# Operand starts on 128-byte multiples and a reordered opening, in a fused two-block kernel

## Chip, core and metric

One core of a Trainium2 chip runs the whole program. The metric is the device time of one launch in microseconds; lower is better.

## The reference, cut to what matters

A sequence of 256 tokens of width 1024 goes through two models, one after the other, each of two layers. Everything is float32. A layer of the first model is a SwiGLU feed-forward, a mixer (retention, stick-breaking attention and a Mamba-2 scan side by side) and a second feed-forward; a layer of the second is a mixer of three attentions and a feed-forward. Each of these stages is preceded by a root-mean-square norm whose gain and shift come from a conditioning vector `c`:

```
mod = (silu(c) @ ada_w[l] + ada_b[l]).reshape(B, 3 * N_SUB, D_MODEL)[:, None]
u = modulate(rmsnorm(h, norm_ffn1[l]), mod[:, :, 0], mod[:, :, 1])
h = h + 0.5 * (1.0 + mod[:, :, 2]) * swiglu(u, ffn1_wg[l], ffn1_wu[l], ffn1_wd[l])
```

So there are ten stages, nearly all of their arithmetic in products of 256 tokens with weight matrices that are read once from HBM, and some 470 MB of weights in all.

## The kernel before, in words

**Products.** A float32 value x is split into H = x rounded to float32r and L = x - H, and a product is three matmuls in float32r (`mm3`, line 174): H·H, H·L, L·H. In a matmul one operand is loaded into the array (128 columns, a weight load, called PEld in the profile) and the other streams past it (up to 512 columns). The profile writes a matmul as out<-streamed,loaded: `A<-s,uH` streams a weight tile `s` past the activations `uH`, `A<-uH,s` streams activations past weights. For the feed-forward, `gemmB` (line 380) and `down` stream 512 weight columns past the activations `uH`/`uL` or `m`; `gemmA` (line 389) streams 256 activation columns. Plain float32 matmuls (attention scores and the like) are done in two passes, and transposes (`tr`, line 179) stream the identity past the tile.

**Weights.** `dma_next` (line 301) loads 512 KB units on SP's queue into tiles of tag s4. `prep_H` copies a unit to float32r on ACT (line 321), `prep_L` subtracts on DVE (line 185). The conditioning products are done on DVE: `ada_load` (line 501) brings 512 KB, `ada_dot` (line 506) multiplies by silu(c) and sums.

**Order.** Python runs the stages once and writes the instructions out in order. `pump` advances a planned clock by 216 ns a matmul and lets side lanes (transposes, attention, ada dots) step when their planned time has come. The opening (`prologue`) is written by hand in the order in which every engine is to run it: two outer products spread c over the partitions and ACT applies silu; the norms of the two halves of x; transposes of x; then for k = 0 to 7 the gain and shift of 128 features, their u, and the products of that k with four weight groups, each into a PSUM bank of its own.

**Memory.** Tiles come from pools, and a pool's tiles have tags. A tag has a fixed number of buffers that lie together; the tags of a pool lie one behind the other in the order of first use, each buffer rounded up to 32 bytes a partition. The constants' pool begins at byte 1152 and holds onesrow 512, h0 and h1 4096 each, vtab 1768 (1792), ident 512, mhalf 32, ctab 10496, ones 4 (32), and onesr, identr, nones 512 each. Behind it come the working tags, before the change in the order s4 (36 of 4096), cb (4096), sm (16 of 32), gs (8 of 32), v8 (3 of 32), uH and uL (8192 each), m2 (15 of 2048), then small ones. Summed up, s4 begins at byte 24256, which is 64 past a multiple of 128; uH, uL and m2 begin 32 past one. Slices of these tiles that go into products step by 512 bytes or multiples, so every s4 operand starts at 64, every u and m2 operand at 32 (modulo 128). `ident` starts at 0, `ltrir` (a small late tag) at 0.

Of the kernel before, what the change touches and what calls it, by code (L numbers as in the profile page):

```python
# [13 lines left out]
AF = mybir.ActivationFunctionType  # L14
ALU = mybir.AluOpType
# [4 lines left out]
D = 1024  # L20
FF = 2816
NJ = FF // 256
EPS = 1e-6
# [80 lines left out]
class K:  # L104
# [196 lines left out]
    def dma_next(self):  # L301
        i = self.dma_i
        k, src = self.plan[i]
        raw = self.m4([128, 1024])
        n = src.shape[1]
        self.nc.sync.dma_start(raw[:, :n], src)
        self.raws[i] = (raw, k, n // k)
        self.dma_i += 1
        self.raw_live += 1
# [5 lines left out]
    def prep_H(self):  # L315
        self.fill_dma()
        raw, k, wd = self.raws.pop(self.prep_i)
        n = k * wd
        H = self.m4([128, 1024], F32R)
        L = self.m4([128, 1024], F32R)  # L320
        self.nc.scalar.copy(H[:, :n], raw[:, :n])  # L321
        vh = H[:, :n].rearrange("p (k n) -> p k n", k=k)
        vl = L[:, :n].rearrange("p (k n) -> p k n", k=k)
        self.prepped[self.prep_i] = (vh, vl)
        self.prep_i += 1
        self.live += 1
        self.last_prep = self.now
        return H, L, raw, n
# [374 lines left out]

    def run(self):
        a, nc = self.a, self.nc
        self.ones_row = self.t([1, 128], "onesrow", 1, pool=self.cst)
        nc.vector.memset(self.ones_row, 1.0)
        crow = self.m4([1, 1024])
        nc.sync.dma_start(crow, a["c"])
        self.h = [self.t([128, 1024], f"h{i}", 1, pool=self.cst) for i in range(2)]  # L710
        x = a["x"].rearrange("o (t p) d -> (o t) p d", p=128)
        for tt in range(2):
            nc.sync.dma_start(self.h[tt], x[tt])
        self.vtab = self.t([128, NV], "vtab", 1, pool=self.cst)
        nc.sync.dma_start(self.vtab, a["vtab"])
        self.ident = self.t([128, 128], "ident", 1, pool=self.cst)
        make_identity(nc, self.ident)
        self.mhalf = self.t([128, 8], "mhalf", 1, pool=self.cst)
        nc.gpsimd.memset(self.mhalf, -0.5)
        self.ctab = self.t([128, NCST], "ctab", 1, pool=self.cst)  # L720

        ph = self.phase_list()
        for plan, _, _, _ in ph:
            plan()

        items = self.ada_plan()
        while items[0][0] != ph[0][2][0]:
            items.pop(0)
        with self.tc.manual_schedule():
            u = self.prologue(crow, items[:2])  # L730
        self.ones = self.t([128, 1], "ones", 1, pool=self.cst)
        nc.gpsimd.memset(self.ones, 1.0)
        self.onesr = self.t([128, 128], "onesr", 1, F32R, pool=self.cst)
        nc.scalar.copy(self.onesr, self.ones.to_broadcast([128, 128]))
        self.identr = self.t([128, 128], "identr", 1, F32R, pool=self.cst)
        nc.scalar.copy(self.identr, self.ident)
        self.nones = self.t([128, 128], "nones", 1, pool=self.cst)
        nc.gpsimd.memset(self.nones, -1.0)
        self.later(60.0, lambda: nc.sync.dma_start(self.ctab, a["ctab"]))
        self.filling = True  # L740
        self.fill_dma()
        self.ada = self.spawn([self.ada_gen(items[2:])], 4.0)
        pend = None

        for i, (_, body, _, gate) in enumerate(ph):
            last = i == len(ph) - 1
            xn = {}
            g = {}
            self.WH = 12 if body == self.ffn else 8
            self.pace = PACE[i]  # L750
            self.ada_ok = True
            for ev, accs in body(u, pend):
                if "gate" not in g:
                    g["gate"] = self.need(*gate)
                if ev in (0, 1):
                    self.hold = True
                    if last:
                        self.finish(ev, accs, g["gate"])
                        continue
                    ex = self.final_mod if ph[i + 1][2][0][0] == "b" and ph[i][2][0][0] == "a" else None  # L760
                    if ex:
                        self.fm = self.fm if hasattr(self, "fm") else self.final_mod_prep()
                    xn[ev] = self.fin_a(ev, accs, g["gate"], ex)
                elif ev == 2 and not last:
                    nu = self.new_u()
                    g["G"], g["S"] = self.need(*ph[i + 1][2][0]), self.need(*ph[i + 1][2][1])
                    self.fin_b(0, xn[0], nu, g["G"], g["S"])
            if not last:
                u = nu
                pend = (lambda xn1, nu, G, Sh: lambda: self.fin_b(1, xn1, nu, G, Sh))(xn[1], nu, g["G"], g["S"])  # L770

    def prologue(self, crow, items):


        nc = self.nc
# [3 lines left out]
        def issue(k, steps):  # L779
            for s in steps:  # L780
                if s == "a":
                    raws[k] = (self.ada_load(wg, k), self.ada_load(ws, k))
                else:
                    self.dma_next()
# [6 lines left out]

        self.cb = self.t([128, 1024], "cb", 1)
        self.cb_of = cn
        for nb in range(2):
            c = slice(nb * 512, nb * 512 + 512)
            p = self.pB()
            self.mm(p, self.ones_row, crow[:, c], True)
            self.act(self.cb[:, c], p, AF.Silu)


        ss = [self.sm([128, 2]) for _ in range(2)]
        xn = [self.m4([128, 1024]) for _ in range(2)]
        for t in ss:
            nc.gpsimd.memset(t, 0.0)
        self.act(xn[0], self.h[0], AF.Square, accum_out=ss[0][:, 0:1])
        nc.vector.scalar_tensor_tensor(xn[1], self.h[1], 1.0, self.h[1], op0=ALU.mult, op1=ALU.mult,
                                       accum_out=ss[1][:, 0:1])
        r = [self.rstd2(t) for t in ss]
        g = self.vtab[:, _VEC["nf1"]:_VEC["cw"]]
        self.ts(g, g, 32.0, ALU.mult)  # L810
        gb = self.t([128, 8], "gs", 8)
# [1 line left out]
        v8 = [self.t([128, 8], "v8", 3) for _ in range(2)]  # L813
        gs = [self.t([128, 8], "gs", 8) for _ in range(2)]

        def dot(k):
            self.ada_dot(raws[k][0], v8[0][:, k:k + 1])

        def scale(k):
            c = slice(k, k + 1)  # L820
            self.act(gs[0][:, c], v8[0][:, c], AF.Identity, scale=gain[:, c], bias=gb[:, c])
# [5 lines left out]
        for tt in range(2):  # L827
            self.act(xn[tt][:, 512:1024], self.h[tt][:, 512:1024], AF.Copy, scale=r[tt])
        xT = [self.m4([128, 4, 256]) for _ in range(2)]
        for q in range(4):  # L830
            p = (self.pT, self.pA)[q // 2]()
            for i in range(4):
                k, tt = q * 2 + i // 2, i % 2
                self.tr(p[:, i * 128:i * 128 + 128], xn[tt][:, k * 128:k * 128 + 128])
            dst = xT[q // 2][:, q % 2 * 2:q % 2 * 2 + 2].rearrange("p k n -> p (k n)")
            nc.scalar.copy(dst, p)

        u = self.new_u()
        self.WH = 12
# [2 lines left out]
        def products(k, j0):  # L842
            W = self.take()
            for b in range(2):
                for tt in range(2):
                    self.mm3(ps[j0 + b][tt], self.uap(u, tt, k), (W[0][:, b], W[1][:, b]), k == 0, k == 7)
            self.done()

        for k in range(8):
            c = slice(k, k + 1)  # L850
            self.ada_dot(raws.pop(k)[1], v8[1][:, c])
            w = self.prep_H()
            self.act(gs[1][:, c], v8[1][:, c], AF.Identity, bias=bs[:, c])
            if k < 7:
                dot(k + 1)
            t = self.m2([128, 2, 128])
            self.act(t, xT[k // 4][:, k % 4].rearrange("p (t n) -> p t n", t=2), AF.Identity, scale=gs[0][:, c],
                     bias=gs[1][:, c])
            nc.scalar.copy(u[0][:, :, k], t)
            self.sub(u[1][:, :, k], t, u[0][:, :, k].bitcast(F32))  # L860
            if k < 7:
                scale(k + 1)
            w2 = self.prep_H()
            self.prep_L(w)
            products(k, 0 if k < 7 else 2)
            self.prep_L(w2)
            products(k, 2 if k < 7 else 0)
            if k + 3 < 8:
                issue(k + 3, "aww")
            else:  # L870
                self.dma_next()
                self.dma_next()
# [973 lines left out]
```

## Time and profile before

| | |
|---|---|
| median of 3 runs | 1977.92 us (1977.2 to 1978.46) |
| the profiled execution | 1974.64 us, of which the span of the profile is 1972.9 us |
| PE busy | 1924.5 us of the span |
| mean granted TensorE clock | 0.996 of 2.4 GHz |
| DMA | 471.18 MB, 239 GB/s on average |

Busy times are of the profiled execution; times in a timeline are from the start of the span. A matmul's duration in the profile is longer than the distance to the next one's start, because matmuls are pipelined: what a matmul costs is that distance, called its pitch here.

### The profile page before, as it was taken

Reading aid. Unit: us, or ns where it says so; the run is one execution under the profiler, and the core shown is the slowest. Engines: PE = TensorE matmul, PEld = TensorE weight load, DVE = VectorE, ACT = ScalarE, POOL = GpSimd, SP = SyncE. Lnnn points to the kernel's source line nnn. Section 1 sums busy time; section 2 is a strip of 40 time slices with the busy share of each in tenths; the row PEclk is TensorE's granted clock in tenths of the full one; section 3 lists DMA queues with packets and bytes.
Section 4 is the critical chain, followed back from the end, with each engine's and each line's share of the span. In section 5 each row is a group of like instructions: output and inputs, shape, how many; then the busy total and the mean of one; then the engine's idle time right before and its main releaser. Section 6 shows DMA issues by size and latency. Waiting matters only on the chain.

```text
span 1972.9 us, 25540 instructions
## 1 busy us (share of the span) xinstructions
PE 1924.5 (98%) x9228; PEld 1559.0 (79%) x9228; DVE 1454.5 (74%) x2239; ACT 995.6 (50%) x1653; POOL 69.8 (4%) x139
## 2 busy tenths in 40 slices
PE   7999999999999999999999999999999999999998
PEld 5788797887887877988878778778788787777886
DVE  6877788787877787687877767678878676788552
ACT  6633556554435444475644445744544357546441
POOL 0000000100000000000100002100000010000000
PEclk9999999999999999999999999999999999999999
DMA  9989585389877896774598766467789763676640
GB/s 368 357 293 347 203 310 182 121 251 354 288 257 271 263 351 238 253 233 143 175 293 281 265 177 174 140 209 266 277 331 299 185 182 117 215 275 221 209 159 22
DMA packets 151344, 471.18 MB, mean 239 GB/s; under 512 B 36657, under 2 KB 36785, under 8 KB 151090
## 3 DMA queue, kind: packets, MB, share of 16 engines
q1 hardware_dynamic: 137010, 463.21, 68.9%
q10 hardware_dynamic: 14208, 6.34, 1.3%
q8 instruction: 72, 1.18, 0.2%
q14 instruction: 54, 0.44, 0.1%
HBM read 468.40 MB, written 1.10 MB: 238 GB/s over the span
## 4 chain that ended last, share of the span: by engine, by line
PE 61%; issue 28%; DVE 6%; DMA 2%; ACT 2%; POOL 1%; ACTq 0%; DVEq 0%; POOLq 0%
PE A L170 40%; PE B L170 18%; PE T L182 3%; DVE s L185 2%; DMA row<-g 1%; DVE m L185 1%; ACT m L206 1%; PE T L170 1%; DVE s L506 1%; DMA s<-in_ada_w 0%; DMA s<-in_ffn_gu 0%; DVE s L203 0%; ACT s L321 0%; POOL sm L229 0%; POOL sm L227 0%
## 5 line engine op out<-in xcount | busy, mean ns | idle before, releaser
L170 PE MATMUL A<-s,uH 128*128 128x512 f32 (+1 forms) x2976 | 952.0, 401 | 4.0 <-ACT uH L214 2.4
L185 DVE TENSOR_TENSOR s<-s,s 128x1024 fp32r<-128x1024 f32 (+2 forms) x638 | 754.5, 1199 | 135.1 <-ACT s L321 130.0
L321 ACT CAST s<-s 128x1024 fp32r<-128x1024 f32 (+1 forms) x618 | 624.1, 1043 | 89.6 <-DVE s L185 31.0
L170 PEld LDWEIGHTS A<-s,uH 128*128 128x128 f32 x2976 | 551.9, 189 | 134.9 <-issue 9.0
L170 PE MATMUL A<-s,uL 128*128 128x512 f32 (+1 forms) x1488 | 589.3, 397 | 1.5 <-DVE uL L185 1.5
L170 PE MATMUL B<-s,m 128*128 128x512 f32 (+2 forms) x1696 | 414.1, 392 | 1.1 <-ACT m L214 0.9
L170 PEld LDWEIGHTS B<-s,m 128*128 128x128 f32 x1696 | 309.9, 189 | 70.5 <-ACT m L214 2.8
L506 DVE SCALAR_TENSOR_TENSOR s<-s,cb 128x1024 f32<-128x1024 f32 x256 | 311.4, 1218 | 49.0 <-DMA s<-in_ada_w 42.1
L170 PEld LDWEIGHTS A<-s,uL 128*128 128x128 f32 x1488 | 281.1, 189 | 69.2 <-DVE uL L185 4.2
L206 ACT ACTIVATE m<-A 128x256 f32<-128x256 f32 x126 | 48.4, 384 | 268.8 <-PE A L170 268.2
L214 ACT CAST m<-T 128x256 fp32r<-128x256 f32 x132 | 48.9, 372 | 221.9 <-PE T L182 213.4
L170 PE MATMUL A<-uH,s 128*128 128x256 f32 (+1 forms) x672 | 129.3, 288 | 2.4 <-ACT s L1400 2.3
L185 DVE TENSOR_TENSOR m<-m,A 128x256 f32<-128x256 f32 x126 | 52.6, 417 | 89.3 <-ACT m L206 88.7
L170 PEld LDWEIGHTS A<-uH,s 128*128 128x128 f32 (+1 forms) x672 | 105.4, 187 | 4.1 <-ACT s L1400 2.8
L170 PE MATMUL B<-s,s 128*128 128x512 f32 (+3 forms) x432 | 103.2, 384 | 0.9 <-ACT s L206 0.5
L182 PE MATMUL T<-ident,m 128*128 128x128 f32 (+1 forms) x488 | 85.4, 276 | 16.5 <-DVE m L185 15.1
L182 PEld LDWEIGHTS T<-ident,m 128*128 128x128 f32 (+1 forms) x488 | 62.9, 140 | 46.8 <-DVE m L185 20.8
L185 DVE TENSOR_TENSOR m<-T,m 128x256 fp32r<-128x256 f32 x132 | 55.2, 420 | 58.7 <-ACT m L214 58.2
L170 PE MATMUL A<-uL,s 128*128 128x256 f32 (+1 forms) x336 | 95.5, 284 | 0.0
L170 PEld LDWEIGHTS B<-s,s 128*128 128x128 f32 (+1 forms) x432 | 78.8, 188 | 16.5 <-DVE s L203 1.2
L206 ACT ACTIVATE m<-h 128x512 f32<-128x512 f32 x44 | 27.8, 632 | 83.8 <-DVE h L185 82.0
L170 PEld LDWEIGHTS A<-uL,s 128*128 128x128 f32 (+1 forms) x336 | 63.4, 189 | 0.7
(188 smaller groups left out, 1199.7 us busy)
## 6 DMA issues: line engine op xcount, KB each, us to landing
s<-in_ffn_gu SPq DMA_DIRECT2D x264, 512.0 KB, 5.5
s<-in_ada_w SPq DMA_DIRECT2D x240, 512.0 KB, 6.6
s<-in_w_in_blk SPq DMA_DIRECT2D x152, 512.0 KB, 5.2
s<-in_ffn_wd SPq DMA_DIRECT2D x88, 512.0 KB, 5.4
s<-in_ffn_w_down SPq DMA_DIRECT2D x44, 512.0 KB, 5.1
s<-in_w_out SPq DMA_DIRECT2D x40, 512.0 KB, 4.3
s<-in_final_ada_w SPq DMA_DIRECT2D x16, 512.0 KB, 9.3
s<-row ACTq DMA_DIRECT2D x12, 512.0 KB, 7.1
```

Source lines behind the costliest of these rows:

```text
L170: self.last = self.nc.tensor.matmul(out, l, r, start=start, stop=stop, skip_group_check=True)
L182: self.nc.tensor.transpose(out, in_, self.ident[:p, :p])
L185: self.nc.vector.tensor_tensor(o, x, y, op=op)
L206: return self.nc.scalar.activation(o, x, f, **kw)
L214: self.nc.scalar.copy(H, x)
L321: self.nc.scalar.copy(H[:, :n], raw[:, :n])
L506: self.nc.vector.scalar_tensor_tensor(raw, raw, 1.0, self.cb, op0=ALU.mult, op1=ALU.mult, accum_out=v)
```

## The change

Three things are done. (1) At the head of `run` one 64-byte constant tile is taken and never used, and one tile each of s4, m2, uH, uL and cb is taken before anything else, so that these tags come first and in this order. By the same sums s4, m2, uH, uL and cb then all begin at multiples of 128, as do onesr, identr and nones; h0, h1, vtab and ident move to 64 past one, ctab to 96, ltrir to 64. (2) The opening is rewritten: one chain gives both reciprocal norms, ACT squares the first half of x between the two silu halves, the four PSUM copies of the transposed x are put behind the first weight's H, and for k = 0 DVE makes u straight from PSUM. (3) The constant table's load is ordered behind the last weight load issued when its lane is stepped, and two constant casts on ACT behind the last prep_H of the opening.

```diff
     def run(self):
+        self.t([128, 16], "pad", 1, pool=self.cst)
+        self.m4([128, 1024]), self.m2([128, 512]), self.new_u(), self.t([128, 1024], "cb", 1)
...
-        nc.scalar.copy(self.onesr, self.ones.to_broadcast([128, 128]))
-        nc.scalar.copy(self.identr, self.ident)
+        with self.act_order(self.last_H):
+            nc.scalar.copy(self.onesr, self.ones.to_broadcast([128, 128]))
+            nc.scalar.copy(self.identr, self.ident)
...
-        self.later(60.0, lambda: nc.sync.dma_start(self.ctab, a["ctab"]))
+        def table():
+            with self.tc.issue_after(self.last_dma.ins):
+                nc.sync.dma_start(self.ctab, a["ctab"])
+        self.later(60.0, table)
...
+        pc = [self.pB() for _ in range(2)]
         for nb in range(2):
-            c = slice(nb * 512, nb * 512 + 512)
-            p = self.pB()
-            self.mm(p, self.ones_row, crow[:, c], True)
-            self.act(self.cb[:, c], p, AF.Silu)
-        ss = [self.sm([128, 2]) for _ in range(2)]
+            self.mm(pc[nb], self.ones_row, crow[:, nb * 512:nb * 512 + 512], True)
+        self.act(self.cb[:, 0:512], pc[0], AF.Silu)
+        ss = self.sm([128, 2])
         xn = [self.m4([128, 1024]) for _ in range(2)]
-        for t in ss:
-            nc.gpsimd.memset(t, 0.0)
-        self.act(xn[0], self.h[0], AF.Square, accum_out=ss[0][:, 0:1])
+        self.act(xn[0], self.h[0], AF.Square, accum_out=ss[:, 0:1])
+        self.act(self.cb[:, 512:1024], pc[1], AF.Silu)
         nc.vector.scalar_tensor_tensor(xn[1], self.h[1], 1.0, self.h[1], op0=ALU.mult, op1=ALU.mult,
-                                       accum_out=ss[1][:, 0:1])
-        r = [self.rstd2(t) for t in ss]
+                                       accum_out=ss[:, 1:2])
+        e = self.sm([128, 2])
+        nc.gpsimd.tensor_scalar(e, ss, D * EPS, None, op0=ALU.add)
+        rr = self.sm([128, 2])
+        nc.gpsimd.tensor_tensor(rr, e, self.mhalf[:, :2], op=ALU.pow)
...
-            dst = xT[q // 2][:, q % 2 * 2:q % 2 * 2 + 2].rearrange("p k n -> p (k n)")
-            nc.scalar.copy(dst, p)
+            px.append(p)
+        def evac(q):
+            nc.scalar.copy(xT[q // 2][:, q % 2 * 2:q % 2 * 2 + 2].rearrange("p k n -> p (k n)"), px[q])
...
+            if k == 0:
+                v = px[0][:, 0:256].rearrange("p (t n) -> p t n", t=2)
+                w = self.prep_H()
+                self.add(gs[1][:, c], v8[1][:, c], bs[:, c])
+                self.ts(t, v, gs[0][:, c], ALU.mult, gs[1][:, c], ALU.add)
+                nc.vector.tensor_copy(u[0][:, :, k], t)
+                for q in range(4):
+                    evac(q)
+            else:
...
             self.sub(u[1][:, :, k], t, u[0][:, :, k].bitcast(F32))
+            if k == 0:
+                self.prep_L(w)
+                w2 = self.prep_H()
+                dot(1)
+                scale(1)
+            else:
...
```

## Rows read from the trace of the kernel before

**Rows 1.** The page, busy time of PE; its group of transposes.
```profile
PE 1924.5 (98%) x9228; PEld 1559.0 (79%) x9228; DVE 1454.5 (74%) x2239; ACT 995.6 (50%) x1653; POOL 69.8 (4%) x139
...
L182 PE MATMUL T<-ident,m 128*128 128x128 f32 (+1 forms) x488 | 85.4, 276 | 16.5 <-DVE m L185 15.1
```
**Rows 2.** Windows: us, busy and count by engine, PEclk, DMA share, GB/s.
```profile
50.00:100.00 50.00, 49.73 (x222) 39.53 (x221) 43.29 (x61) 32.24 (x51) 0.00 (x0) 1.00 0.94 351
100.00:150.00 50.00, 50.00 (x221) 40.19 (x220) 37.06 (x56) 17.89 (x26) 0.00 (x0) 1.00 0.81 302
...
850.00:900.00 50.00, 50.00 (x290) 42.87 (x289) 45.12 (x79) 31.17 (x50) 3.80 (x12) 1.00 0.55 191
...
1200.00:1250.00 50.00, 46.71 (x265) 38.38 (x264) 40.42 (x98) 32.28 (x76) 15.06 (x26) 0.97 0.56 173
...
1450.00:1500.00 50.00, 50.00 (x222) 40.17 (x221) 40.58 (x60) 20.23 (x28) 0.00 (x0) 1.00 0.94 353
```
**Rows 3.** Groups of PE by form: out<-streamed,loaded, count, busy us, mean ns.
```profile
L170 PE MATMUL A<-s,uH 128*128 128x512 f32 x2912 | 934.4, 402 | 4.0 <-ACT uH L214 2.4 <-DVE m L185 1.3 <-DVE m L1513 0.2
L170 PE MATMUL A<-s,uL 128*128 128x512 f32 x1456 | 578.1, 398 | 1.5 <-DVE uL L185 1.5
L170 PE MATMUL B<-s,m 128*128 128x512 f32 x1584 | 397.4, 400 | 1.1 <-ACT m L214 0.9
L170 PE MATMUL A<-uH,s 128*128 128x256 f32 x640 | 123.9, 289 | 2.4 <-ACT s L1400 2.3
...
L170 PE MATMUL B<-s,s 128*128 128x512 f32 x336 | 82.3, 395 | 0.9 <-ACT s L206 0.5 <-DVE s L203 0.3
...
L170 PE MATMUL A<-s,s 128*128 128x512 f32 x240 | 59.7, 396 | 0.0
```
**Rows 4.** Timeline of PE, five stretches: start us, us from first to last.
```profile
234.72 0.39 PE L170 MATMUL A<-s,uL 128*128 128x512 f32 x1
...
238.93 0.40 PE L170 MATMUL A<-s,uL 128*128 128x512 f32 x1
...
246.04 0.40 PE L170 MATMUL A<-uH,s 128*128 128x256 f32 x2
...
251.81 0.40 PE L170 MATMUL A<-uH,s 128*128 128x256 f32 x2
...
342.28 0.62 PE L170 MATMUL B<-m,ltrir 128*128 128x512 f32 x2
342.74 0.64 PE L170 MATMUL A<-s,uH 128*128 128x512 f32 x2
...
1289.96 1.89 PE L170 MATMUL B<-s,s 96*128 96x256 f32 x8
1291.69 0.60 PE L182 MATMUL T<-ident,m 128*128 128x128 f32 x4
...
1318.15 11.08 PE L170 MATMUL A<-s,s 128*128 128x512 f32 x48
1329.07 0.62 PE L170 MATMUL A<-s,uH 128*128 128x512 f32 x2
```
**Rows 5.** Chain that ended last, the opening: start us, us, what.
```profile
9.07 1.25 POOL sm L227
...
11.54 1.76 PE T L182 x7
...
15.04 0.58 ACT s L836
...
19.48 2.93 PE B L170 x6
```
**Rows 6.** Timeline of the opening, DVE's first dot: start us, us.
```profile
8.65 1.23 DVE L506 SCALAR_TENSOR_TENSOR s<-s,cb 128x1024 f32<-128x1024 f32 x1 [1.03 <-DMA s<-in_ada_w]
```
**Rows 7.** Timeline, one matmul and the weight load behind it.
```profile
599.96 0.63 PE L170 MATMUL A<-s,uH 128*128 128x512 f32 x2
599.96 0.19 PEld L170 LDWEIGHTS A<-s,uH 128*128 128x128 f32 x1
```

More of the change, by code (lines that the diff above doesn't have):

```diff
@@ L305, in dma_next @@
         n = src.shape[1]
-        self.nc.sync.dma_start(raw[:, :n], src)
+        self.last_dma = self.nc.sync.dma_start(raw[:, :n], src)
         self.raws[i] = (raw, k, n // k)
@@ L320, in prep_H @@
         L = self.m4([128, 1024], F32R)
-        self.nc.scalar.copy(H[:, :n], raw[:, :n])
+        self.last_H = self.nc.scalar.copy(H[:, :n], raw[:, :n])
         vh = H[:, :n].rearrange("p (k n) -> p k n", k=k)
@@ L793, in prologue @@
         self.cb_of = cn
+        pc = [self.pB() for _ in range(2)]
         for nb in range(2):
-            c = slice(nb * 512, nb * 512 + 512)
-            p = self.pB()
-            self.mm(p, self.ones_row, crow[:, c], True)
-            self.act(self.cb[:, c], p, AF.Silu)
-        ss = [self.sm([128, 2]) for _ in range(2)]
+            self.mm(pc[nb], self.ones_row, crow[:, nb * 512:nb * 512 + 512], True)
+        self.act(self.cb[:, 0:512], pc[0], AF.Silu)
+        ss = self.sm([128, 2])
         xn = [self.m4([128, 1024]) for _ in range(2)]
-        for t in ss:
-            nc.gpsimd.memset(t, 0.0)
-        self.act(xn[0], self.h[0], AF.Square, accum_out=ss[0][:, 0:1])
+        self.act(xn[0], self.h[0], AF.Square, accum_out=ss[:, 0:1])
+        self.act(self.cb[:, 512:1024], pc[1], AF.Silu)
         nc.vector.scalar_tensor_tensor(xn[1], self.h[1], 1.0, self.h[1], op0=ALU.mult, op1=ALU.mult,
-                                       accum_out=ss[1][:, 0:1])
-        r = [self.rstd2(t) for t in ss]
+                                       accum_out=ss[:, 1:2])
[3 more added lines that the diff above has]
+        nc.gpsimd.tensor_tensor(rr, e, self.mhalf[:, :2], op=ALU.pow)
+        r = [rr[:, tt:tt + 1] for tt in range(2)]
         g = self.vtab[:, _VEC["nf1"]:_VEC["cw"]]
@@ L829, in prologue @@
         xT = [self.m4([128, 4, 256]) for _ in range(2)]
+        px = []
         for q in range(4):
@@ L851, in prologue @@
             self.ada_dot(raws.pop(k)[1], v8[1][:, c])
[L852 to L855, printed above, removed]
             t = self.m2([128, 2, 128])
-            self.act(t, xT[k // 4][:, k % 4].rearrange("p (t n) -> p t n", t=2), AF.Identity, scale=gs[0][:, c],
-                     bias=gs[1][:, c])
-            nc.scalar.copy(u[0][:, :, k], t)
-            self.sub(u[1][:, :, k], t, u[0][:, :, k].bitcast(F32))
[L861 to L864, printed above, removed]
+            if k == 0:
[7 more added lines that the diff above has]
+            else:
+                w = self.prep_H()
+                self.act(gs[1][:, c], v8[1][:, c], AF.Identity, bias=bs[:, c])
+                dot(k + 1) if k < 7 else None
+                self.act(t, xT[k // 4][:, k % 4].rearrange("p (t n) -> p t n", t=2), AF.Identity, scale=gs[0][:, c],
+                         bias=gs[1][:, c])
+                nc.scalar.copy(u[0][:, :, k], t)
+            self.sub(u[1][:, :, k], t, u[0][:, :, k].bitcast(F32))
+            if k == 0:
[4 more added lines that the diff above has]
+            else:
+                if k < 7:
+                    scale(k + 1)
+                w2 = self.prep_H()
+                self.prep_L(w)
             products(k, 0 if k < 7 else 2)
```

## The prediction

> **What bounds the kernel now.** I read the busy times first: PE is busy for 1924.5 us of the span of 1972.9 [rows 1]. A busy PE need not be PE at its peak, so the next view is the windows: in the middle of a feed-forward PE shows 50.00 busy of 50.00 us at full granted clock while DVE has 37.06 and ACT 17.89 [rows 2]. No wait ends late there; what sets the time is how close one matmul follows another. So the third view is the timeline of PE alone, for the pitch, and this is where the answer lies. 512 columns at 2.4 GHz take 213.3 ns. In a stretch of 18 matmuls that stream weights past u, starts go from 234.72 to 238.93: 4.21 / 18 = 0.234 us each [rows 4]. Where the loaded operand is a tile of tag s, 48 matmuls take from 1318.15 to 1329.07: 10.92 / 48 = 0.2275 us [rows 4]. Same engine, same shape, same clock, same streamed tag; only the loaded operand's start differs, 32 past a multiple of 128 bytes in the first, 64 in the second. The groups by form say the same with mean durations of 398 to 402 ns for loaded u and m and 395 to 396 for loaded s [rows 3]. So starts matter, by 7 ns at least, and 14 to 21 ns of every matmul are not columns. The plain float32 products give a floor: eight two-pass matmuls of 256 columns stream for the same 213.3 ns at half the bytes per time, and follow each other by (1291.69 - 1289.96) / 8 = 0.216 us with streamed and loaded operand both at 64 [rows 4].
>
> **The change part by part.**
>
> *Starts of operands.* Afterwards every streamed and loaded operand of the float32r products starts at 0. No float32r matmul of before with 512 columns has both there, so the pitch must be bounded. From below: 216 ns, the row just named, in which nothing but columns and 3 ns is paid. From above: loaded operand at 0 and streamed operand at 32 occurs with ltrir, (342.74 - 342.28) / 2 = 0.230 us [rows 4]; only two matmuls, so 227 to 230. Above 234 nothing lies unless the new starts collide (a rival). I take 216. The reason is the size of what is left: 227 is 213.3 plus 13.5 ns or 32 columns, and 32 columns of 4 bytes are 128 bytes, so a streamed operand of 2048 bytes that starts inside a 128-byte piece touches 17 pieces in place of 16, and 17/16 of 213.3 is 226.7. That the half-rate stream, at the same start of 64, does not pay it fits: it has time to spare for a 17th piece. The gemmA products with u streamed at 32 go at (251.81 - 246.04) / 48 = 0.120 us for 106.7 ns of columns [rows 4], also 13 ns over; they speak for a fixed loss rather than for 17/16, which is why the chance below is not higher.
>
> The price: loaded u and m, 2912 + 1456 + 1584 = 5952 matmuls [rows 3], 234 to 216 is 18 ns each: 107.1 us. Loaded s, 336 + 240 = 576 [rows 3], 227.5 to 216: 6.6 us. gemmA, 640 with uH [rows 3], 120 to 109 (106.7 plus the same 2.5): 7.0 us. Smaller forms are left out. Sum 120.7 us.
>
> *What of it stays.* Not all PE time given back is span. DMA: in 50 to 100 and 1450 to 1500 us the engines are busy for 0.94 of the time at 351 and 353 GB/s [rows 2]; a PE faster by 8% would ask for 1.01, so in such a window (I count seven of the forty) about 1 us of 4 is lost: 7 us. DVE: 45.12 of 50 us in the window at 850 [rows 2]; 50 us of PE cut to 46 leaves it 2% of room, lost 1 us. Seams: the windows of the second model's mixers, as 1200 to 1250 with PE 46.71 [rows 2], are already held by chains through DVE and ACT that do not shrink; there are six like it, with 3 us each at stake: half lost, 9 us. And PE's idle 48.4 us (1972.9 - 1924.5) [rows 1] lie at such seams and grow a little. I put the loss at 17 us, with ends 5 and 40. So 104 us stay.
>
> *Identity.* ident moves to a start of 64 and is streamed in every transpose. The cover is the weight load that each transpose needs. Taken at nothing; if a transpose paid the 7 ns seen between two starts above, 488 of them [rows 1] cost 3.4 us, which is in the range.
>
> *Opening.* Now POOL makes one reciprocal norm after the other, the second from 9.07 on; transposes run from 11.54, ACT copies them out until 15.04 + 0.58, then makes the first H and u, and steady products start at 19.48 [rows 5]. Afterwards both norms come out of one chain, over 1 us sooner (POOL's 1.25), but DVE is then held by its first dot, which waits for a load until 8.65 and takes 1.23 [rows 6]: the scaled x is ready about 0.7 us earlier, no more. The four copies of 0.58 leave the front of ACT's queue, so the first H can be made when ACT has done its own scaling, at about 11.7, and DVE makes t, uH and uL of k = 0 from PSUM (three operations of some 0.4 us) before L: L is then done at about 14.6 (an estimate from these rows), and products are steady there and not at 19.48. The gain is 4.8 us, say 5. What is behind these on their queues: DVE's dot for k = 1 comes after L and not before it, and its result is needed only when 24 matmuls have run. Ends: 2.3 us if only the four copies count, 7 if PE, with less of a pause between transposes and products, also has its full clock sooner.
>
> *Table and casts.* 1.3 MB leave SP's queue ahead of k = 3's loads; the table is first read in the first mixer, a whole feed-forward later. Taken at nothing, as part of the above; it is what lets loads keep up with earlier products. If they don't, the opening gains the lower end.
>
> **Sum.** Against the profiled execution: 1974.64 - 104 - 5 = 1865.6. That execution was 3.3 us below the median of the runs, so about 1868.
>
> A rule that speaks against this: the Trainium skill, SBUF — State Buffer, Door 1, says that SBUF has lines of 16 bytes and that each crossing into a new line costs. Starts at 32, 64 and 0 are all on such lines, so by that alone the pitches stay and the sum would be 1977.9 - 5 = 1973. The 234 against 227 above disagrees with it already.
>
> **Rivals.**
>
> *The loaded operand alone counts.* Then 227 is the best there is (a fixed 13 ns of float32r) and only the step from 234 goes: 5952 x 7 = 41.7 us, some 37 after losses, with the opening 42: 1936. With ltrir's 230 it is 5952 x 4 - 576 x 2.5 = 22.4, with the opening 25 after losses: 1952. For it: 227 is seen where u is streamed at 32 too (the 13 ns of gemmA). Against: the half-rate products at the same starts do not pay. The same time would come if the change did not do what it says, the unused tile taking no place: all tags would then start at 64, the row of 0.2275.
>
> *Nothing from starts, the opening alone* (the rule of the Trainium skill above would have it so). 7 ns between loaded u and loaded s could come from which tag it is and not from where it starts. Then 1973. Against: mean, clock and shape agree in all other things.
>
> *Slower: both operands in step.* A weight load starts at the same 599.96 as the matmul that it runs beside [rows 7]. If streamed and loaded operand, both at 0, ask for the same piece in the same moment, each matmul could lose another step like that from 227 to 234, and more: 234 to 241 for 5952 and 227 to 241 for 576 is 41.7 + 7.8 = 49.5 us, less the opening's 5: 2022. It decides from 0.8 ns a matmul on (5 us over 6528). For it: starts do interact, and the row with loaded 0 (230) is slower than that with 64 (227). Against: in those of 227 both start at 64, equally in step, and they are the fastest of the float32r rows. The Trainium skill, SBUF — State Buffer, Who interferes with whom, gives PE two read ports of its own for the two, by which this costs nothing; no run here shows the ports.
>
> **Chances.** About 0.2% (4 us) is what a measurement of this kernel tells from no change. Both starts count, down to about 216: 0.54, time 1868, own range 1845 (no seams lost, opening 7) to 1892 (loss 40). The loaded alone: 0.32, 1930 to 1952. Opening alone: 0.07, at the edge between faster and same. In step: 0.07. The range takes in the first two, nearly whole, 1845 to 1950. Faster 0.88, same 0.05, slower 0.07.
>
> **What would show it.** In the timeline the pitch of A<-s,uH and B<-s,m falls from 0.234 to 0.216, A<-s,s to the same; the windows of the feed-forwards hold some 238 matmuls in 50 us where they hold 221; transposes keep their durations. In the opening steady products start near 14.6. DMA shares reach 0.97 and more in the windows that have 0.94. Wrong: a pitch of 227 in all (the first rival), or of 240; or a pitch of 216 with PE idle far beyond 48 us, which would say that another engine took over.

## The result and the profile after

The changed kernel takes 1950.95 us (median, 1949.93 to 1953.95); the kernel before, on the same chip, 1978.19 us. The ratio is 0.9853, with a 95% interval of 0.9819 to 0.9888. The forecast was 1868 with a range up to 1950: the sign was right, the size was not, 27 us of gain where 110 were forecast. The profiled execution took 1949.93 us, with a span of 1948.2 us.

First the page of the changed kernel, its span and its busy times.

```profile
span 1948.2 us, 25535 instructions
...
PE 1888.2 (97%) x9228; PEld 1555.2 (80%) x9228; DVE 1452.8 (75%) x2242; ACT 991.4 (51%) x1649; POOL 68.7 (4%) x135
```

PE is busy for 36.3 us less than in [rows 1], but its idle time grew from 48.4 to 60.0 us. So the span fell by 24.7 us only. Next its groups by form, the answer to [rows 3] (count, busy us, mean ns, idle before).

```profile
L170 PE MATMUL A<-s,uH 128*128 128x512 f32 x2912 | 918.5, 396 | 4.5 <-ACT uH L214 2.4 <-DVE m L185 1.7 <-DVE m L1542 0.2
...
L170 PE MATMUL B<-s,m 128*128 128x512 f32 x1584 | 388.9, 395 | 0.7 <-ACT m L214 0.5
...
L170 PE MATMUL B<-s,s 128*128 128x512 f32 x336 | 82.2, 394 | 0.9 <-ACT s L206 0.5 <-DVE s L203 0.3
```

The mean of the products with loaded uH and m fell by 6 and 5 ns; that of B<-s,s, which was at the short pitch before, did not move. The timeline of PE gives the pitch, as in [rows 4].

```profile
225.57 0.39 PE L170 MATMUL A<-s,uL 128*128 128x512 f32 x1
...
228.31 0.39 PE L170 MATMUL A<-s,uL 128*128 128x512 f32 x1
...
1301.87 10.37 PE L170 MATMUL A<-s,s 128*128 128x512 f32 x45
```

The first two rows lie 12 matmuls apart: 2.74 / 12 = 0.228 us, against 0.234 before. The 45 of the last row go at (10.37 - 0.39) / 44 = 0.227 us, against 0.2275. Over some 6200 neighbouring pairs of 512-column float32r products, the mean distance of starts is 227.8 ns (before: 234.2 over some 5700 pairs with loaded u or m, 227.8 over some 500 with loaded s). **All float32r products of 512 columns now have the pitch that those with loaded s had.** None of them went to 216.

The windows, as in [rows 2] (us, busy and count by engine, PEclk, DMA share, GB/s), with two more in which PE lost time:

```profile
50.00:100.00 50.00, 49.62 (x227) 40.33 (x226) 44.89 (x62) 31.29 (x50) 0.00 (x0) 1.00 0.92 348
100.00:150.00 50.00, 50.00 (x228) 41.18 (x227) 35.88 (x55) 18.81 (x27) 0.00 (x0) 1.00 0.81 305
200.00:250.00 50.00, 44.44 (x249) 37.87 (x248) 38.27 (x60) 25.24 (x43) 2.76 (x4) 0.93 0.70 248
...
1450.00:1500.00 50.00, 50.00 (x227) 41.19 (x226) 40.79 (x58) 22.72 (x32) 0.00 (x0) 1.00 0.88 309
1500.00:1550.00 50.00, 42.91 (x184) 34.80 (x183) 30.32 (x45) 16.68 (x26) 0.86 (x2) 0.90 0.73 212
```

A feed-forward window holds 228 matmuls where it held 221; the forecast was 238. In the windows at 200 and 1500 PE is idle for 5.6 and 7.1 us, and the granted clock is 0.93 and 0.90, that is, some 7 and 10 of the 50 us at the lower level of 1.2 GHz. In the trace's clock records the stretches at that level, without the one at the very end, sum to 27.3 us, against 13.7 before (the records of before start at 23.4 us, those of after at 14.5).

PE's largest waits after (what waited for what: us in total, times, longest us), then the same line before:

```profile
PE T L182 <- DVE m L185: 28.0, 14, 7.1
```
```profile
PE T L182 <- DVE m L185: 15.1, 11, 3.6
```

These are transposes of a gated product `m`; four gaps after (5.34 us near 207, 5.39 near 1001, 2.49 near 1133 and 7.06 near 1528) make up 20.3 of the 28.0 us. They are called seams here. This one line explains 12.9 us, all of the growth of PE's idle time and a little more.

**A ledger.** Pitch: 5952 matmuls by 6.4 ns is 38.1 us. Idle time took back 11.6. The 13.6 us more at the lower clock cost at most half of themselves, 6.8 us; less than that, since in before the products from 20.08 to 23.06 us, where it has no record yet, go at 0.427 us each, which is 512 columns at the lower level (`align_only` has the same pitches there, and a granted clock of 0.50 from 20 to 24 us). That leaves 19.7 to 26.5 us, and the span fell by 24.7. Set against each other at the same matmul, the traces show it step by step: in the feed-forwards after gains 0.95 us in every 150 matmuls; in the mixers nothing; and at four seams it loses 2.4 us (near 200 us), 1.9 (1000), 3.7 (1140) and 3.5 (1530).

### The profile page after: what moved, and what is told of

It reads as the page before. It is cut to its first block, busy times and chain, and to the rows that moved or that the text cites. A ratio compares the mean times of both kernels' runs of the same rounds, so it can differ in the third digit from the quotient of the medians.

```text
span 1948.2 us, 25535 instructions
## 1 busy us (share of the span) xinstructions
PE 1888.2 (97%) x9228; PEld 1555.2 (80%) x9228; DVE 1452.8 (75%) x2242; ACT 991.4 (51%) x1649; POOL 68.7 (4%) x135
## 4 chain that ended last, share of the span: by engine, by line
PE 59%; issue 28%; DVE 6%; DMA 4%; ACT 2%; POOL 1%; SPq 0%; ACTq 0%; DVEq 0%; POOLq 0%
PE A L170 39%; PE B L170 17%; PE T L182 3%; DVE s L185 2%; DMA row<-g 2%; DMA s<-in_ada_w 1%; DVE m L185 1%; ACT m L206 1%; ACT s L321 1%; DMA s<-in_ffn_wd 1%; DVE s L506 1%; DMA s<-in_ffn_gu 1%; DVE s L203 1%; DVE sm L1696 0%; DVE h L185 0%
## 5 line engine op out<-in xcount | busy, mean ns | idle before, releaser
L170 PE MATMUL A<-s,uH 128*128 128x512 f32 (+1 forms) x2976 | 936.2, 395 | 4.5 <-ACT uH L214 2.4
L170 PE MATMUL A<-s,uL 128*128 128x512 f32 (+1 forms) x1488 | 581.5, 392 | 0.3 <-DVE uL L185 0.3
L170 PE MATMUL B<-s,m 128*128 128x512 f32 (+2 forms) x1696 | 405.6, 387 | 0.7 <-ACT m L214 0.5
L185 DVE TENSOR_TENSOR m<-T,m 128x256 fp32r<-128x256 f32 x132 | 55.1, 420 | 56.8 <-ACT m L214 56.5
```

The source lines that it names most:

```text
L170: self.last = self.nc.tensor.matmul(out, l, r, start=start, stop=stop, skip_group_check=True)
L185: self.nc.vector.tensor_tensor(o, x, y, op=op)
```

## Experiments

The first four and the two probes were run once each. Of these the pitch and the waits at one seam are read, not the time: the first four shared a chip with a kernel before that took 1995.07 us there.

### Which starts matter: four layouts

All four have the changed kernel's order of instructions; only the starts differ. In `all64` s4, u and m2 all start 64 past a multiple of 128 bytes, in `all32` all 32 past one. In `s0u64` s4 starts at 0 and u and m2 at 64; in `s64u0` the other way round.

```diff
 all64
-        self.t([128, 16], "pad", 1, pool=self.cst)
 all32
-        self.t([128, 16], "pad", 1, pool=self.cst)
+        self.t([128, 24], "pad", 1, pool=self.cst)
 s0u64
-        self.m4([128, 1024]), self.m2([128, 512]), self.new_u(), ...
+        self.m4([128, 1024]), self.t([128, 16], "gap", 1), self.m2([128, 512]), self.new_u(), ...
 s64u0
-        self.t([128, 16], "pad", 1, pool=self.cst)
-        self.m4([128, 1024]), self.m2([128, 512]), self.new_u(), ...
+        self.m4([128, 1024]), self.t([128, 16], "gap", 1), self.m2([128, 512]), self.new_u(), ...
```

> The changed kernel without its 64-byte pad: s4, m2, uH, uL and cb all start 64 past a multiple of 128. In step (what counts is that the streamed and the loaded operand have the same start modulo 128): pitch of A<-s,uH 227 ns, time 1951 us within 3. Loaded operand alone, at a multiple of 64: 227 and 1951 as well. Multiples of 128 (both at 0): over 230 ns and 1965 us or more.

> Pad of 96 bytes: all five tags start 32 past a multiple of 128. In step: 227 ns and 1951 us. Loaded alone, at a multiple of 64: 234 ns and some 1983 us. Multiples of 128: over 230 ns.

> 64 bytes more between s4 and m2: weights at 0, u, m2 and cb at 64. In step: A<-s,uH and B<-s,m 230 to 236 ns (after the change m streamed at 0 past ltrir at 64 went at 232 to 236), A<-s,s 227, time 1970 to 1990 us. Loaded alone, at a multiple of 64: 227 and 1951 us. Multiples of 128: over 230.

> No pad, 64 bytes between s4 and m2: weights at 64, u, m2 and cb at 0. In step: A<-s,uH and B<-s,m 230 to 236 ns, time 1970 to 1990 us. Loaded alone: 227 and 1951 us. Multiples of 128: over 230.

Measured, PE's timeline in a feed-forward. First `all64`:

```profile
227.50 0.39 PE L170 MATMUL A<-s,uL 128*128 128x512 f32 x1
...
229.55 0.39 PE L170 MATMUL A<-s,uL 128*128 128x512 f32 x1
```

Nine matmuls in 2.05 us: 0.228. Then `s0u64`:

```profile
227.44 0.39 PE L170 MATMUL A<-s,uL 128*128 128x512 f32 x1
...
230.93 0.40 PE L170 MATMUL A<-s,uL 128*128 128x512 f32 x1
```

Fifteen in 3.49 us: 0.233. And `s64u0`:

```profile
225.17 0.40 PE L170 MATMUL A<-s,uL 128*128 128x512 f32 x1
...
227.97 0.39 PE L170 MATMUL A<-s,uL 128*128 128x512 f32 x1
```

Twelve in 2.80 us: 0.233. Means over all such pairs, in ns (start of the streamed operand / of the loaded one, modulo 128 bytes):

| | 0/0 | 64/64 | 32/32 | 64/32 | 0/64 | 64/0 |
|---|---|---|---|---|---|---|
| 512 columns | 227.8 | 227.8 | 227.8 | 234.2 | 233.2 | 233.2 |
| kernel | after | all64 | all32 | before | s0u64 | s64u0 |

**What follows.** It is not the multiple of 128 that counts but whether both operands start in step, that is, at the same offset. In both mixed layouts A<-s,s, which is in step with itself, stayed at 228. The change works because it brings u and m2 into step with s4; leaving the pad out does the same. One thing is not told apart: these slices step by 512 bytes, so operands in step had the same start modulo 512 too, and whether the same start modulo 128 would do is not shown. The 96 products of 416 columns, whose streamed slices step by 1664 bytes, gain nothing: 189.6 ns after, 187.9 before.

For the 256-column products of `gemmA` it is otherwise: 119.8 ns in step (after), 119.9 before at 32/64, and 116.5 in both mixed layouts. A shift of 64 helps them, one of 32 does nothing. `s` is loaded there and streamed in the others, so one start of `s` can't serve both; a second tag was not tried.

### What is left above the columns: two probes

`probe` is the changed kernel with eight rows of 24 products at its end, all in step; they add work to PE and nothing to the outputs. `probe2` shifts the loaded operand instead.

```diff
 probe
+        for s, l, n, c in ((ws, wl, 512, 128), (bs, bl, 512, 128), (ws, wl, 384, 128), (ws, wl, 256, 128),
+                           (ws, wl, 512, 32), (ws, wl, 512, 8), (bs, bl, 512, 8), (bs, bl, 256, 128)):
+            for i in range(24):
+                nc.tensor.matmul(p[i % 2][:c, :n], l[:, i % 4 * 128:i % 4 * 128 + c], s[:, i % 2 * 512:i % 2 * 512 + n], ...)
 probe2
+        for s, l, n, so, lo in ((ws, wl, 512, 0, 0), (ws, wl, 512, 0, 8), (ws, wl, 512, 0, 16), (ws, wl, 512, 0, 24),
+                                (ws, wl, 512, 8, 8), (ws, wl, 512, 0, 4), (bs, bl, 512, 0, 32), (ws, wl, 256, 0, 16)):
+            for i in range(24):
+                nc.tensor.matmul(p[i % 2][:, :n], l[:, i % 3 * 128 + lo:i % 3 * 128 + lo + 128],
+                                 s[:, i % 2 * 256 + so:i % 2 * 256 + so + n], ...)
```

(ws and wl are float32r, bs and bl bfloat16; so and lo count elements.)

> The changed kernel with eight rows of 24 matmuls behind its last product, all operands at 0: float32r 512 columns, bfloat16 512, float32r 384 and 256, float32r 512 with 32 and with 8 loaded columns, bfloat16 512 with 8 loaded columns, bfloat16 256. A fixed cost of float32r: 227, 216, 173.5, 120, and 220 to 227 with few loaded columns; bfloat16 216 and 109 whatever is loaded. A cost of the weight load beside it, whatever the type: bfloat16 227 too, and about 216 with few loaded columns in both types. A rate of 16/17 in float32r: 226.7, 170, 113.3.

> The changed kernel with eight rows of 24 products at its end, whose loaded operand is shifted against the streamed one: 512 columns of four bytes with shifts 0, 32, 64, 96 bytes, both shifted by 32, loaded by 16; 512 columns of two bytes with shift 64; 256 columns of four bytes with shift 64. If equal starts modulo 128 bytes are what counts: 227 ns with shift 0 and with both shifted by 32; 230 with a shift of 32, 233 to 234 with 64, something between for 96, and for 16 more than 227. If the absolute start counts, both shifted by 32 is slower than shift 0. The 256 columns: 116 with the shift, 120 without. Two bytes: 216 if only four-byte operands feel it.

Measured in `probe`, the timeline of PE cut inside each row (start, us from the first start to the last end, loaded shape, streamed shape, count):

```profile
1939.61 4.47 PE L919 MATMUL A<-s,s 128*128 128x512 f32 x19
1944.60 4.48 PE L919 MATMUL A<-s,s 128*128 128x512 bf16 x20
1950.27 2.93 PE L919 MATMUL A<-s,s 128*128 128x384 f32 x16
1954.33 1.84 PE L919 MATMUL A<-s,s 128*128 128x256 f32 x14
1956.83 4.56 PE L919 MATMUL A<-s,s 128*32 128x512 f32 x19
...
1967.79 4.48 PE L919 MATMUL A<-s,s 128*8 128x512 bf16 x20
1973.29 1.91 PE L919 MATMUL A<-s,s 128*128 128x256 bf16 x16
```

A matmul's own duration comes off the end (0.39, 0.38, 0.34, 0.28, 0.39, 0.38 and 0.27 us): 4.08 / 18 = 0.227 for float32r, 4.10 / 19 = 0.216 for bfloat16; 0.173 and 0.120 for 384 and 256 columns; 0.232 with only 32 loaded columns; and for bfloat16 again 0.216 with 8 loaded columns and 0.109 with 256 streamed ones. Float32r pays some 11 ns more than bfloat16 at 512 and at 256 columns alike. Over their columns (213.3, 160 and 106.7 ns) the three float32r rows in step pay 13.4, 13 and 13 ns: **a fixed cost for each matmul in step**, not a share of its columns, which at 17/16 would be 13.3, 10 and 6.7. Nor does a smaller weight load lift it: with 32 or 8 loaded columns the pitch was higher, not lower.

`probe2` shows how small a shift is enough. First both at 0, then the loaded one moved by 32, 64 and 96 bytes, both moved by 32, the loaded one moved by 16; then bfloat16 moved by 64, and 256 columns moved by 64.

```profile
1943.69 4.24 PE L919 MATMUL A<-s,s 128*128 128x512 f32 x18
1948.46 4.82 PE L919 MATMUL A<-s,s 128*128 128x512 f32 x20
1954.28 4.59 PE L919 MATMUL A<-s,s 128*128 128x512 f32 x19
1959.65 4.61 PE L919 MATMUL A<-s,s 128*128 128x512 f32 x19
1965.72 4.27 PE L919 MATMUL A<-s,s 128*128 128x512 f32 x18
1970.74 5.06 PE L919 MATMUL A<-s,s 128*128 128x512 f32 x21
1976.77 4.05 PE L919 MATMUL A<-s,s 128*128 128x512 bf16 x18
1981.76 2.21 PE L919 MATMUL A<-s,s 128*128 128x256 f32 x18
```

In the same way: 0.226, 0.233, 0.233, 0.234, 0.228, 0.2335, 0.216 and 0.1135 us. Any shift costs about 6.6 ns, 16 bytes as much as 64; the 230 expected for a shift of 32 was a miss. Both moved together is as fast as both at 0 once steady (the row's last 14 distances are 226 or 227 ns). Bfloat16 does not feel the start, and the 256 columns gain 6 ns from this shift of 64.

### One part alone

`align_only` is the kernel before with the pad and the five early tiles; `open_only` is the changed kernel without them.

```diff
 align_only: the kernel before
+        self.t([128, 16], "pad", 1, pool=self.cst)
+        self.m4([128, 1024]), self.m2([128, 512]), self.new_u(), self.t([128, 1024], "cb", 1)
 open_only: the changed kernel
-        self.t([128, 16], "pad", 1, pool=self.cst)
-        self.m4([128, 1024]), self.m2([128, 512]), self.new_u(), self.t([128, 1024], "cb", 1)
```

> The kernel before with the pad and the five early tiles alone; the order of instructions is that of before. Starts as the source of the gain: pitch 227 ns, 6.4 ns less for some 6,200 matmuls, 39 us, less 6 to 12 us at the seams: 1945 to 1955 us if the first seam (which has the order of before here) is not lost, that is about the changed kernel's time without its opening. Opening as the source: 1975 us.

> The changed kernel without the pad and the five early tiles: starts as before. Starts as the source: pitch 234 ns, opening 3 to 5 us earlier, of which the changed order at the first seam gives back 2 or more: 1973 to 1978 us. Opening as the source: 1955 us.

Against the kernel before at 1980.53 us on the same chip: `align_only` 1950.95 us, ratio 0.9852 (0.9828 to 0.9877); `open_only` 1981.47 us, ratio 1.0008 (0.9992 to 1.0024). The starts carry the whole gain, and the opening none that can be measured.

Why, when the opening did start its products sooner? PE's last product of the opening (the 192nd) in `open_only`, after, and before:

```profile
64.96 0.40 PE L170 MATMUL B<-s,uL 128*128 128x512 f32 x1
```
```profile
62.24 0.39 PE L170 MATMUL B<-s,uL 128*128 128x512 f32 x1
```
```profile
65.93 0.40 PE L170 MATMUL B<-s,uL 128*128 128x512 f32 x1
```

At the old pitch 1.0 us of the opening's lead is left at that point, and the first seam takes more than that. Every traced kernel with the new opening (after, `open_only`, `late_row`, `row_pool`, the four layouts, the two probes) has a gap of 5.0 to 5.4 us on PE near 210 us; in the three with the old one (before, `align_only`, `al_late`) none there exceeds 1.25 us. Matmul by matmul, the profiled execution of `open_only` (1983.53 us) then loses 2.8 us against before near 200 us, at the first seam, where the order of the side lanes comes out differently, and 3.6, 3.0 and 3.7 us at seams near 870, 1035 and 1180, with pitches unchanged between them. Its ten times run from 1973.73 to 1988.18 us, so the later losses probably differ from run to run; only one of its runs is traced, so this is not shown.

### The seam near 1528 us

`ada_fin` writes a gate row to DRAM (line 550, `row<-g`) and reads it back spread over the partitions (line 554, `s<-row`), both from ACT's queue. The changed kernel there, timeline (ACTq is ACT's queue issuing; brackets: idle before, and for what):

```profile
1502.79 0.41 ACTq L550 DMA_DIRECT2D row<-g  x1
...
1520.23 0.34 ACTq L554 DMA_DIRECT2D s<-row  x1
1520.62 0.37 ACT L214 CAST m<-T 128x256 fp32r<-128x256 f32 x1 [11.61 <-DMA row<-g]
...
1528.14 0.69 PE L182 MATMUL T<-ident,m 128*128 128x128 f32 x2 [7.06 <-DVE m L185]
```

And before the change:

```profile
1523.18 0.38 ACTq L550 DMA_DIRECT2D row<-g  x1
...
1537.83 0.34 ACTq L554 DMA_DIRECT2D s<-row  x1
1538.21 0.37 ACT L214 CAST m<-T 128x256 fp32r<-128x256 f32 x1 [8.48 <-DMA row<-g]
...
1545.74 0.47 PE L182 MATMUL T<-ident,m 128*128 128x128 f32 x1 [3.56 <-DVE m L185]
```

From one issue to the other it is 14.7 us before and 17.4 us after, no less with the faster PE; ACT holds the second issue, and everything behind it, until then. The Trainium skill, DMA: Bandwidth & Descriptors, section "Anatomy of one DMA — SWDGE (gpsimd) path", says that a semaphore wait happens on the issuing sequencer before dispatch; these rows agree, with 11.61 and 8.48 us of a still ScalarE.

How much of the longer gap is due to the faster PE? `probe2` is the changed kernel up to its last product, and has this there:

```profile
1510.61 0.41 ACTq L550 DMA_DIRECT2D row<-g  x1
...
1524.40 0.34 ACTq L554 DMA_DIRECT2D s<-row  x1
...
1532.31 0.44 PE L182 MATMUL T<-ident,m 128*128 128x128 f32 x2 [3.38 <-DVE m L185]
```

The row takes 13.8 us here and the gap is 3.38 us; in `probe`, the same code up to there, they are 16.4 and 5.99, in `align_only` 14.4 and 4.03. In all of these and in `open_only` (14.0 and 2.91) PE goes on 7.91 or 7.92 us after the second issue, as it does in the two views above. So the gap is the row's time less a stretch that PE's own work covers: 10.4 us at the new pitch (after, both probes, `align_only`) and 11.1 at the old (before, `open_only`). Of the 3.5 us that the changed kernel loses at this seam, the faster PE accounts for 0.7. The other 2.8 are a row that took longer in the profiled execution, 17.44 us against 14.65; that is chance of the run as far as these traces tell, and why the row's time varies stays open.

Three kernels test what the wait itself does: `late_row` (from the changed kernel) and `al_late` (from `align_only`) issue the second transfer later in the order; `row_pool` (from the changed kernel) leaves it where it is and issues it from GpSimd's queue.

```diff
 late_row, al_late
-            yield 6.0
+            yield 14.0
 row_pool
-            self.nc.scalar.dma_start(g, row.to_broadcast([128, 1024]))
+            self.nc.gpsimd.dma_start(g, row.to_broadcast([128, 1024]))
```

> The changed kernel with the second gate DMA of each vector (the one that waits for the first to land, on ACT's queue) planned 8 us later. ACT's queue as the cause of the seam at 1528 us: ACT no longer stands still for 11.6 us, PE's wait of 7.1 us there goes and the granted clock stays up: 5 to 9 us less, 1942 to 1946 us. If DVE or the loads hold that seam anyway: 1950 us within 2.

> The changed kernel with the spreading transfer of the gate's row on GpSimd's queue instead of ScalarE's, at its old place in the program. If what costs 7 us at the seam near 1528 is ScalarE waiting in its queue for the row's landing, that gap is gone without any later issue: 1940 to 1946 us, ScalarE's wait of 11.6 us on the row not there. If the seam is limited by the row's landing itself (the gate comes late for whoever needs it), the gap stays: 1949 to 1953. A rival that costs: GpSimd is slow to issue the transfer and the gate comes later still, gaps before the multiplies that need it, over 1953.

> The kernel before with its operands in step, the opening untouched, and the transfer that spreads the gate's row issued later. If the opening is worth nothing and the seam near 1530 is ScalarE's queue held by that transfer: about 1943 us, ratio 0.979 to 0.983, within 3 us of the changed kernel with the same late transfer. If the new opening carries part of the gain: 1947 or more. The 4.0 us gap of the tensor engine near 1526 in the aligned kernel is gone in both cases; pitch of the 512-column products 227.7 ns.

| kernel | us | ratio to before | PE idle, us |
|---|---|---|---|
| changed | 1950.95 | 0.9853 (0.9819 to 0.9888) | 60.0 |
| row_pool | 1946.56 | 0.9852 (0.9830 to 0.9873) | 55.1 |
| late_row | 1943.06 | 0.9803 (0.9776 to 0.9831) | 56.3 |
| align_only | 1950.95 | 0.9852 (0.9828 to 0.9877) | 57.3 |
| al_late | 1933.83 | 0.9790 (0.9773 to 0.9806) | 47.1 |

The times come from different chips, on which the kernel before takes 1978.19 us (changed), 1980.53 (`late_row`, `align_only`) and 1976.13 (`row_pool`, `al_late`); compare the ratios.

The window of `late_row` around that seam, then the timeline of `row_pool`:

```profile
1500.00:1550.00 50.00, 49.56 (x222) 39.52 (x221) 37.81 (x58) 22.64 (x38) 1.05 (x3) 1.00 0.81 239
```
```profile
1521.36 0.53 POOL L554 DMA_DIRECT2D s<-row  x1 [101.36 <-DVE s L185]
1528.69 1.23 DVE L506 SCALAR_TENSOR_TENSOR s<-s,cb 128x1024 f32<-128x1024 f32 x1 [4.74 <-DMA s<-in_ada_w]
...
1532.59 0.44 PE L182 MATMUL T<-ident,m 128*128 128x128 f32 x2 [2.32 <-DVE m L185]
```

In `late_row` PE is busy for 49.56 us of this window instead of 42.91, at full granted clock instead of 0.90. In `row_pool` the second issue still waits until 1521.36, but GpSimd waits now, not ScalarE; ScalarE's 11.61 us are gone and PE's gap is 2.32 us, ended by a modulation load that DVE waits for. That the 7.06 us gap is ScalarE held in its queue is shown. What it is worth by itself is not: `row_pool`'s ratio is that of the changed kernel, and the 5 us or more that were expected of it did not come.

For the late issue the proof is `al_late`: its interval lies below that of `align_only`, 0.6% or some 12 us. Not all of it is this seam. The later issue also shifts the side lanes, and the seam near 1000 us, where `align_only` has a gap of 4.66 us, has one of 2.07 us; gaps of 1.94 and 2.65 us near 441 and 682 us have no counterpart above 1.5 us. Nor need all of it come from the starts and the issue together: at the seam near 1540 of the kernel before, `al_late` gains some 4 us on that kernel, whose own gap of 3.56 us there is gone too. The late issue on the kernel before was not run, so what it is worth there is open. `al_late` against `late_row` says once more that the opening brings nothing: their intervals overlap, and the kernel with the old opening has the lower median. `al_late` has the lowest ratio here, though not clear of `late_row`: the starts of the change, the opening of before, one constant.

Its page:

```profile
span 1931.1 us, 25544 instructions
...
PE 1884.0 (98%) x9228; PEld 1550.0 (80%) x9228; DVE 1452.7 (75%) x2239; ACT 994.7 (52%) x1653; POOL 70.0 (4%) x139
```

PE's idle time is 47.1 us, about as before the change, and the span is 41.8 us shorter. So with PE's idle time held where it was, a gain the size of the whole pitch term of 38.1 us, and a little more, reaches the span.

## Why the prediction was wrong, by its steps

**What bounds the kernel: right.** The pitch of the matmuls set the time, the starts of operands set part of the pitch, and the row pair of 0.234 against 0.2275 in [rows 4] told it.

**Starts of operands, 216 ns: wrong, and the step that failed.** It took the floor from the half-rate float32 rows and explained 227 by 17 pieces of 128 bytes in place of 16. Three runs refute that: with both operands at 0 (after), where the streamed one touches 16 pieces, at 64 and at 32, where it touches 17, the pitch is the same 227.8; and `probe` shows the rest as fixed, 11 ns at 256 and at 512 columns. The prediction had the row that said so, `gemmA` at 0.120 for 106.7 [rows 4], and named it as speaking for a fixed loss; it should have decided, being a float32r row, where the half-rate row was another kind of matmul. 216 is real, but for bfloat16. The Trainium skill, TensorE: Matmul & The Clock Gate, "Wait — 56ns, not 53.3ns?", gives the columns plus about 2.5 ns, 215.7 for 512: the bfloat16 rows of `probe` agree with 0.216, the float32r rows, at 0.227, do not. Of the term, 107.1 us became 38.1, the 6.6 for loaded s became nothing, and so did the 7.0 for `gemmA` (119.9 to 119.8 ns; there are 960 of these, the prediction counted the 640 with uH).

**First rival, the loaded operand alone: right in its number, wrong in its mechanism.** It had a pitch of 227 and, with the losses, 1936, or 1952 with ltrir's 230; the pitch came out as the first and the time near the second, because the opening brought nothing and the seams took more. But loaded 64 with streamed 0 goes at 233 (`s0u64`), and loaded 0 with streamed 64 too (`s64u0`), so the loaded start alone does not decide; that its time lies near 1952 is luck.

**Slower rival, both in step: the right variable with the wrong sign.** The operands do interact through their relative start, but for these products it is the coincidence that is fast. The argument against it in the prediction, that the fastest float32r rows were in step already, was the whole answer. By the two read ports that the Trainium skill, SBUF — State Buffer, "Who interferes with whom", gives PE, starts should cost nothing relative to each other; 227 against 233 does not agree.

**Nothing from starts: wrong**, by 0.9852 for `align_only`.

**What stays, 17 us lost: the seams too small, the DMA part not put to the test.** At 227 the DMA share is 0.92 and 0.88 in the windows that had 0.94, and PE is busy for 49.62 and 50.00 us of them, so the 7 us did not arise, nor did the 1 us of DVE; what they would be at 216 no run shows. The seams were put at 9 us; the four losses sum to 11.5, and they are not in the second model's mixers, where the prediction put them. The one near 200 comes with the new opening. At 1528 it is a gate row that ScalarE waits for: 0.7 us with the faster PE, 2.8 with the longer row of that run. At 1000 DVE waits 6.95 us for a modulation load, 3.83 before. What sets the one near 1140 was not tried.

**Opening, 5 us: wrong at the end of the chain.** Its own steps came close: the first weight's L is done at 14.09 and products are steady from 14.63, where 14.6 was forecast for both. But 19.48, which the prediction took for the first steady product, is only the second; this is the third in the kernel before:

```profile
20.08 0.63 PE L170 MATMUL B<-s,uL 128*128 128x512 f32 x1
```

There the products go on at 0.427 us until 23.06, in the changed kernel at 0.227 at once. So the lead is 5.4 us at the third product and 7.1 at the 25th (26.74 against 19.62), the upper end that the prediction gave for a full clock sooner. The timeline of the changed kernel shows what came next.

```profile
14.63 0.39 PE L170 MATMUL B<-s,uL 128*128 128x512 f32 x1
...
20.82 0.50 PE L170 MATMUL B<-s,uH 128*128 128x512 f32 x1 [0.81 <-DVE s L185]
...
26.76 1.23 DVE L506 SCALAR_TENSOR_TENSOR s<-s,cb 128x1024 f32<-128x1024 f32 x1 [3.70 <-DMA s<-in_ada_w]
```

PE had overtaken the loads: DVE waits for a modulation load, and PE is idle for 2.96 us at 29.5. Of the 7.1 us at the 25th product 3.7 are left at the 192nd, 1.2 of them from the new pitch (192 by 6.4 ns), and `open_only` has 1.0. The prediction had said that the opening gives its lower end if loads don't keep up, but did not look up when the loads of k = 3 and later land.

**Identity and table at nothing: no run speaks against it.** The transposes keep their mean of 276 ns, with the same count.

## What to carry to other kernels

In float32r products of 512 columns, let the streamed and the loaded operand start at the same offset (here modulo 512 bytes; whether 128 would do was not told apart). A shift of 16 bytes already costs 6 to 7 ns a matmul. At 256 columns a shift of 64 bytes is faster, and at 416 nothing was gained, so measure the shape that the kernel has. Take the floor of a pitch from a row of the same data type, and read a fixed loss off two sizes of the same type. Look for transfers that wait in the queue of an engine that others need, and before a longer gap is put down to a faster engine, see in a second run of the same code how much it varies.

## What was not expected of the hardware

- Streamed and loaded operand interact through their relative start: 227 ns in step, 233 to 234.5 with shifts of 16 to 96 bytes (512 columns, float32r); 120 in step and 113.5 (`probe2`) or 116.5 (in the kernel) with a shift of 64 (256 columns); 216 in bfloat16 with or without a shift.
- In step a float32r matmul has a pitch some 11 ns longer than a bfloat16 one (227 against 216 at 512 columns, 120 against 109 at 256). Over the columns themselves several means come near steps of 6.67 ns, the time of 16 columns: 6.8 (256 columns, shifted), 13.3 (in step), 19.9 (512 columns, shifted). Others do not (9.8 for the 116.5 above), and what is behind it stays open.
- Fewer loaded columns made float32r in step slower: 0.232 us with 32 where 128 have 0.227. Why is open too.
- Writing a 4 KB gate row (line 550) took from 13.8 us (`probe2`) to 17.4 us (after) from its issue to the issue of the transfer that needed it, at the same place of the same code.
